# Attention with its split differences on VectorE, a shorter reciprocal square root and squares summed by ScalarE

## The chip, the cores and the metric

The kernel runs on one core of a Trainium2 chip. A core has a matrix engine (TensorE, PE in the profile; PEld is its weight load), three engines for arithmetic on whole tiles (VectorE or DVE, ScalarE or ACT, GpSimd or POOL) and a queue engine (SyncE, SP). Each works through its own instructions in order and waits on semaphores for the others. The metric is the device time of one execution in microseconds (us); lower is better.

## What is computed

Two layers over 512 tokens of width 1024, in fp32. Each layer is half a SwiGLU block, a mixer, and half a SwiGLU block, all behind RMS norms. The first mixer is a gated MLP. The second, which the change is about, is differential attention with 8 heads; every head has two queries and two keys of 64 and a value of 128:

```python
scores = jnp.einsum('bqhcd,bkhcd->bhcqk', qb, k).astype(jnp.float32) * scale   # scale = 64 ** -0.5
p = jax.nn.softmax(jnp.where(mask, scores, neg), axis=-1)
a = p[:, :, 0] - lam * p[:, :, 1]
o = jnp.einsum('bhqk,bkhe->bqhe', a, v)
...
o = rmsnorm(o, subln_g) * (1.0 - lambda_init)          # per head
return o.reshape(B, S, N_HEADS * V_DIM) @ w_o
```

with `rmsnorm(x, g) = x * rsqrt(mean(x*x) + 1e-6) * g`.

## The kernel before

Activations lie feature by token: 8 tiles `hT` of 128 features by 512 tokens. To keep fp32 accuracy at the speed of the fast matmul type, every operand is split: a rounded high part, copied by ScalarE (`split`, L166), and a low part, the operand minus its high part (L167). `mm3` (L171 to L173) then does three matmuls for a product: high by high, high by low, low by high. Weights come by DMA from the SP queue into `src` tiles and are split by `weights`, whose argument `engine` says who does the subtraction at L167: VectorE everywhere, except in attention, where three calls (the query weights `wq`, and both halves of the output weights `wo_b`) give it to GpSimd.

Stages run one after the other: a feed-forward block, the mixer, a feed-forward block, the projection of keys and values (`kv_proj`), a feed-forward block, attention, a last feed-forward block. At each border a `Norm` sums squares (GpSimd or VectorE, L217), `sums` brings them to 128 partitions with four small matmuls (`nps`, L222) and computes a reciprocal square root of 128 by 4 numbers with `rsqrt`, and `spread` broadcasts that with matmuls (`rps`, L234). `rsqrt` before: a shift (L179), a multiply-add (L182) and three Newton steps of three instructions (L187, L189, L193): eleven VectorE instructions. Apart from the border it is used once in the mixer, and once for each head in attention, in `subnorm`.

In `attention` the work is cut into 24 units: 8 heads by three groups of query blocks. The program is written as a loop over units with lags (`LAGS`), so that a unit's scores are issued while earlier units are transposed and multiplied by the values. Between them PE gets fill work: the query projections of the heads to come (`qps`, L171 to L173) and, late, the first half of the output projection (`dps`). For one head:

- `query`: VectorE scales the projection by the norm (L832) into one buffer `t1` (`r` in the rows; a ring of one place), ScalarE writes two high copies (L840, four casts of 64 by 512), GpSimd the low part `ql` (L841, two subtractions of 64 by 512).
- `scores`: matmuls into `sc` (L860, L865), a mask (L869), VectorE takes the row maxima (L877) and multiplies them by minus the scale (L879, `nm`), ScalarE takes the exponentials with their sums (L885), VectorE joins the two maps (L890, L892, L896, `pt`).
- `transposed` and `values`: PE transposes (`aps`, L907), ScalarE copies (L912), PE multiplies by the values into `ops` (L919).
- `subnorm`: ScalarE squares 128 by 512 (L930, `osq`), VectorE sums them (L932), divides twice by the softmax sum (L928, L935), scales (L938), does the eleven instructions of `rsqrt`, one product (L943, `rr`) and scales the output (L945, `on`).
- `headed`: PE transposes `on` (`otp`, L954), ScalarE and VectorE split the result (L956, L957).

A scheduler sets the order of the instructions on each engine from the order of the program and from durations of its own; a change of instructions can move others.

Of the kernel before, what the change touches and what calls it, by code (L numbers as in the profile page):

```python
# [9 lines left out]
F32 = mybir.dt.float32  # L10
# [7 lines left out]
P = 128  # L18
# [10 lines left out]
HD = 64  # L29
# [28 lines left out]
def trunk(ctx: ExitStack, tc: tile.TileContext, ins, out: bass.AP):  # L58
# [117 lines left out]
    def rsqrt(x, n, name, keep="ry"):  # L176
        y = sp.tile([P, n], F32, tag="ry", name=name, bufs=4)
        i = sp.tile([P, n], I32, tag="ri", name=name + "i")
        nc.vector.tensor_scalar(  # L179
            out=i, in0=x.bitcast(I32), scalar1=1, scalar2=None, op0=ALU.logical_shift_right  # L180
        )
        nc.vector.tensor_scalar(  # L182
            out=y.bitcast(I32), in0=i, scalar1=-1.0, scalar2=float(0x5F3759DF), op0=ALU.mult, op1=ALU.add
        )
        for step in range(3):
            a = sp.tile([P, n], F32, tag="ra", name=name + "a")
            nc.vector.tensor_tensor(out=a, in0=y, in1=y, op=ALU.mult)  # L187
            b = sp.tile([P, n], F32, tag="rb", name=name + "b")
            nc.vector.scalar_tensor_tensor(  # L189
                out=b, in0=a, scalar=-0.5, in1=x, op0=ALU.mult, op1=ALU.mult  # L190
            )
            z = sp.tile([P, n], F32, tag=keep if step == 2 else "ry", name=name + "z", bufs=4)
            nc.vector.scalar_tensor_tensor(  # L193
                out=z, in0=b, scalar=1.5, in1=y, op0=ALU.add, op1=ALU.mult
            )
            y = z
        return y
# [600 lines left out]
    def attention(nxt, kk, vv, rest, after):  # L798
        with phase("at", 2) as ap:
# [30 lines left out]
            def query(o):  # L830
                t1 = ring_1()
                nc.vector.tensor_tensor(out=t1, in0=o, in1=norm.rb, op=ALU.mult)  # L832
# [3 lines left out]
                for c in range(2):  # L836
# [4 lines left out]
                    nc.gpsimd.tensor_tensor(  # L841
# [5 lines left out]
            def scores(h, qis, l0):  # L847
# [24 lines left out]
                for slot, qi in enumerate(qis):  # L872
                    nk = (qi + 1) * P
                    ks = slice(slot * 256, slot * 256 + nk)
                    mx = sp.tile([P, 2], F32, tag="mx", name="mx")
                    for c, s in enumerate(sc):
                        nc.vector.tensor_reduce(out=mx[:, c : c + 1], in_=s[:, ks], axis=AX.X, op=ALU.max)  # L877
                    nm = sp.tile([P, 2], F32, tag="nm", name="nm")
                    nc.vector.tensor_scalar(  # L879
                        out=nm, in0=mx, scalar1=-(HD ** -0.5), scalar2=None, op0=ALU.mult  # L880
                    )
# [83 lines left out]
            def queries():  # L965

                for h in range(2, HEADS):
                    if h % 2 == 0:
                        pieces = weights(ins["wq"][h // 2], KD, engine=nc.gpsimd)
# [213 lines left out]
```

## Time and profile before

| | |
|---|---|
| median of 3 timed runs | 2111.07 us (2110.56 to 2114.93) |
| the profiled execution: time, span | 2116.63 us, 2114.5 us |
| PE busy, share of the span | 2049.0 us, 97% |
| VectorE busy | 1566.1 us, 74% |
| ScalarE busy | 917.4 us, 43% |
| GpSimd busy | 151.5 us, 7% |
| attention | from about 1575 us to 1735 us of the span |

[...]

### The profile page before, as it was taken

The numbers are of one execution on the slowest core, as the hardware profiler recorded it, in microseconds if no ns is written. First come the engines' busy times: TensorE is split into PE (matmuls) and PEld (weight loads), VectorE is DVE, ScalarE is ACT, GpSimd is POOL, SyncE is SP. The second block draws the span as 40 slices with busy tenths as digits, with TensorE's granted clock in tenths as the row PEclk, the third lists the DMA queues.
The fourth block names the chain that finished last, engine by engine and source line by source line (L and its number), as shares of the span: only waits on it lengthen the run. The fifth ranks groups of instructions, "written<-read, shape, count | busy, mean of one in ns | idle before, by whom it ended". The sixth has DMA issues, their size and how long they took to land.

```text
span 2114.5 us, 31293 instructions
## 1 busy us (share of the span) xinstructions
PE 2049.0 (97%) x12916; PEld 1839.1 (87%) x12916; DVE 1566.1 (74%) x2062; ACT 917.4 (43%) x1203; POOL 151.5 (7%) x131
## 2 busy tenths in 40 slices
PE   6999999999999999999998999999998999999997
PEld 6989898888888889899997899998976778989897
DVE  8868778447554688778688478696867978869687
ACT  6525345323232355335355245352546645525243
POOL 0000002004100000000002000000043320000000
PEclk9999999999999999999999999999998999999998
DMA  4422323332222232423223534242350021423231
GB/s 143 141 86 92 120 75 124 119 102 93 91 92 92 81 100 91 130 80 130 80 90 111 183 105 131 79 130 82 115 186 21 31 100 61 139 71 129 81 102 48
DMA packets 63439, 214.57 MB, mean 101 GB/s; under 512 B 7200, under 2 KB 9376, under 8 KB 63296
## 3 DMA queue, kind: packets, MB, share of 16 engines
q1 hardware_dynamic: 58752, 197.16, 28.5%
q0 software_dynamic: 4400, 15.34, 2.1%
q8 instruction: 101, 1.65, 0.3%
q14 instruction: 42, 0.34, 0.0%
q10 hardware_dynamic: 144, 0.07, 0.0%
HBM read 204.15 MB, written 8.39 MB: 101 GB/s over the span
## 4 chain that ended last, share of the span: by engine, by line
PE 69%; issue 18%; DVE 9%; ACT 2%; DMA 1%; POOL 0%; DVEq 0%; SPq 0%; POOLq 0%; ACTq 0%
PE ra L379 12%; PE rc L379 8%; PE dps L172 8%; PE dps L171 8%; PE dps L173 8%; PE rd L379 4%; PE rb L379 4%; PE ups L172 2%; PE ups L173 2%; PE vps L678 2%; PE ups L171 2%; PE vps L676 2%; PE vps L677 2%; DVE wlo L167 2%; PE sps L711 1%
## 5 line engine op out<-in xcount | busy, mean ns | idle before, releaser
L166 ACT CAST whi<-src 128x1024 fp32r<-128x1024 f32 (+2 forms) x500 | 513.3, 1034 | 870.2 <-PE dps L172 344.2
L167 DVE TENSOR_TENSOR wlo<-src,whi 128x1024 fp32r<-128x1024 f32 (+1 forms) x486 | 584.6, 1210 | 161.2 <-ACT whi L166 160.0
L379 PE MATMUL ra<-r,whi 128*128 128x256 f32 x2112 | 384.7, 282 | 14.8 <-ACT r L276 10.4
L172 PE MATMUL dps<-gl,whi 128*128 128x512 f32 x880 | 343.6, 391 | 2.9 <-DVE gl L167 2.9
L171 PE MATMUL dps<-gh,whi 128*128 128x512 f32 x880 | 344.4, 392 | 0.5 <-ACT r L912 0.4
L173 PE MATMUL dps<-gh,wlo 128*128 128x512 f32 x880 | 343.1, 390 | 0.0
L379 PEld LDWEIGHTS ra<-r,whi 128*128 128x128 f32 x2112 | 325.4, 189 | 19.1 <-ACT r L276 10.9
L379 PE MATMUL ra<-r,wlo 128*128 128x256 f32 x1056 | 296.9, 282 | 3.8 <-DVE wlo L167 3.7
L379 PE MATMUL rc<-r,whi 128*128 128x256 f32 x1408 | 255.1, 281 | 2.0 <-ACT whi L166 1.0
L370 DVE TENSOR_TENSOR src<-src 128x1024 f32<-128x1024 f32 x176 | 215.3, 1223 | 39.5 <-DMA src<-in_gu 36.1
L379 PEld LDWEIGHTS rc<-r,whi 128*128 128x128 f32 x1408 | 216.3, 189 | 4.5 <-DVE k L477 2.8
L379 PEld LDWEIGHTS ra<-r,wlo 128*128 128x128 f32 x1056 | 199.8, 189 | 5.7 <-DVE wlo L167 5.2
L172 PEld LDWEIGHTS dps<-gl,whi 128*128 128x128 f32 x880 | 166.0, 189 | 37.3 <-DVE gl L167 3.3
L379 PE MATMUL rc<-r,wlo 128*128 128x256 f32 x704 | 197.5, 280 | 0.9 <-DVE wlo L167 0.9
L171 PEld LDWEIGHTS dps<-gh,whi 128*128 128x128 f32 x880 | 165.6, 188 | 35.6 <-ACT gh L166 1.4
L173 PEld LDWEIGHTS dps<-gh,wlo 128*128 128x128 f32 x880 | 166.0, 189 | 34.5
L571 DVE TENSOR_TENSOR dps<-dps,rbh 128x512 f32<-128x512 f32 x88 | 61.3, 697 | 120.6 <-PE dps L173 120.5
L379 PEld LDWEIGHTS rc<-r,wlo 128*128 128x128 f32 x704 | 133.3, 189 | 1.1 <-DVE wlo L167 1.1
L379 PE MATMUL rd<-r,whi 128*128 128x256 f32 x704 | 129.4, 282 | 4.4 <-ACT r L276 2.1
L379 PE MATMUL rb<-r,whi 128*128 128x256 f32 x704 | 128.9, 282 | 0.4 <-ACT whi L166 0.4
L379 PEld LDWEIGHTS rd<-r,whi 128*128 128x128 f32 x704 | 108.9, 190 | 5.8 <-DVE r L277 2.5
L379 PEld LDWEIGHTS rb<-r,whi 128*128 128x128 f32 x704 | 109.3, 191 | 0.7 <-ACT whi L166 0.7
(239 smaller groups left out, 3159.6 us busy)
## 6 DMA issues: line engine op xcount, KB each, us to landing
src<-in_gu SPq DMA_DIRECT2D x176, 512.0 KB, 3.4
src<-in_dn SPq DMA_DIRECT2D x64, 512.0 KB, 4.6
src<-in_dn SPq DMA_DIRECT2D x32, 384.0 KB, 3.6
src<-in_wv SPq DMA_DIRECT2D x24, 512.0 KB, 3.5
src<-in_wu SPq DMA_DIRECT2D x24, 512.0 KB, 3.5
src<-in_wo_a SPq DMA_DIRECT2D x24, 512.0 KB, 3.5
src<-in_wk SPq DMA_DIRECT2D x8, 512.0 KB, 3.7
src<-in_wvv SPq DMA_DIRECT2D x8, 512.0 KB, 3.3
```

Of the source, the lines that this page charges most:

```text
L166: nc.scalar.copy(out=hi, in_=src)
L167: engine.tensor_tensor(out=lo, in0=src, in1=hi.bitcast(F32), op=ALU.subtract)
L171: nc.tensor.matmul(o, w[0], x[0], start=start, stop=False)
L172: nc.tensor.matmul(o, w[0], x[1], start=False, stop=False)
L173: nc.tensor.matmul(o, w[1], x[0], start=False, stop=stop)
L370: nc.vector.tensor_tensor(out=out, in0=a, in1=b, op=ALU.add)
L379: nc.tensor.matmul(o[:, a * H : (a + 1) * H], l[:, a, kp, :], r, start=first and kp == 0 and a == 0 and n == 0, stop=False, skip_group_che ...
L571: nc.vector.tensor_tensor(out=o, in0=o, in1=norm.rbh[:, tokens], op=ALU.mult)
L676: nc.tensor.matmul(acc[n], xh[:, ts], hi[:, kk, :], start=k == 0, stop=False)
L677: nc.tensor.matmul(acc[n], xh[:, ts], lo[:, kk, :], start=False, stop=False)
L678: nc.tensor.matmul(acc[n], xl[:, ts], hi[:, kk, :], start=False, stop=k == KD - 1)
L711: nc.tensor.matmul(sps[:, n * P : (n + 1) * P], v[ct // NCH * NCH + n][:, ct % NCH * P : (ct % NCH + 1) * P], wsT[:, gr, :], start=True, s ...
```

## The change

- The three weight loads of attention and the low part of the queries leave GpSimd for VectorE. GpSimd has no arithmetic left in attention.
- The scale of the scores moves from the maxima and the exponential into `query` (L832 becomes one instruction with two multiplications). The maxima are taken negated, straight into `nm`; the multiplication L879 falls away, 32 instructions.
- `rsqrt` takes eight instructions in place of eleven: a start by one multiply-add on the bits, one cubic step, one Newton step. This holds for every norm.
- `subnorm`: four squares of 128 by 128 with sums by ScalarE in place of one of 128 by 512 and a VectorE sum; the divisions by the softmax sum and the final product fall away, since the epsilon is multiplied by that sum squared instead (`el`, one instruction).

```diff
-    def rsqrt(x, n, name, keep="ry"):
-        y = sp.tile([P, n], F32, tag="ry", name=name, bufs=4)
-        i = sp.tile([P, n], I32, tag="ri", name=name + "i")
-        nc.vector.tensor_scalar(
-            out=i, in0=x.bitcast(I32), scalar1=1, scalar2=None, op0=ALU.logical_shift_right
+    C2, C1, C0 = 0.39755464, -1.29562372, 1.89804978
+
+    def rsqrt(x, n, name, keep="rr"):
...
+        y = step(
+            "ry",
+            lambda out: nc.vector.tensor_scalar(
+                out=out.bitcast(I32), in0=x.bitcast(I32), scalar1=-0.5, scalar2=float(0x5F350000),
+                op0=ALU.mult, op1=ALU.add,
+            ),
         )
-        nc.vector.tensor_scalar(
-            out=y.bitcast(I32), in0=i, scalar1=-1.0, scalar2=float(0x5F3759DF), op0=ALU.mult, op1=ALU.add
-        )
-        for step in range(3):
...
+        h = times(times(y, y, "ra"), x, "ra")
+        z = stt(stt(h, C1 / C2, h, ALU.add, "rb"), C0 / C2, y, ALU.add, "ry")
+        b = stt(times(z, z, "ra"), -0.5 * C2**3, x, ALU.mult, "rb")
+        return stt(b, 1.5 * C2, z, ALU.add, keep, bufs=4)
...
             def query(o):
                 t1 = ring_1()
-                nc.vector.tensor_tensor(out=t1, in0=o, in1=norm.rb, op=ALU.mult)
+
+                nc.vector.scalar_tensor_tensor(
+                    out=t1, in0=o, scalar=HD ** -0.5, in1=norm.rb, op0=ALU.mult, op1=ALU.mult
+                )
...
-                    nc.gpsimd.tensor_tensor(
+                    nc.vector.tensor_tensor(
                         out=ql[hs, :], in0=t1[hs, :], in1=qt[hs, :].bitcast(F32), op=ALU.subtract
                     )
...
-                    mx = sp.tile([P, 2], F32, tag="mx", name="mx")
+                    nm = sp.tile([P, 2], F32, tag="nm", name="nm")
                     for c, s in enumerate(sc):
-                        nc.vector.tensor_reduce(out=mx[:, c : c + 1], in_=s[:, ks], axis=AX.X, op=ALU.max)
-                    nm = sp.tile([P, 2], F32, tag="nm", name="nm")
-                    nc.vector.tensor_scalar(
-                        out=nm, in0=mx, scalar1=-(HD ** -0.5), scalar2=None, op0=ALU.mult
-                    )
+                        nc.vector.tensor_reduce(
+                            out=nm[:, c : c + 1], in_=s[:, ks], axis=AX.X, op=ALU.max, negate=True
+                        )
...
             def subnorm(o, l0):
 
-                rl = sp.tile([P, NCH], F32, tag="rl4", name="rl4")
-                nc.vector.reciprocal(out=rl, in_=l0)
+
                 sq = qp.tile([P, T], F32, tag="sq", name="osq").rearrange("p (n e) -> p n e", n=NCH)
-                nc.scalar.activation(out=sq.rearrange("p n e -> p (n e)"), in_=o, func=AF.Square)
                 ss = sp.tile([P, NCH], F32, tag="ss", name="ss")
-                nc.vector.tensor_reduce(out=ss, in_=sq, axis=AX.X, op=ALU.add)
-                for _ in range(2):
-                    st = sp.tile([P, NCH], F32, tag="ss", name="ss")
-                    nc.vector.tensor_tensor(out=st, in0=ss, in1=rl, op=ALU.mult)
-                    ss = st
+                for n in range(NCH):
+                    nc.scalar.activation(
+                        out=sq[:, n, :], in_=o[:, n * P : (n + 1) * P], func=AF.Square, accum_out=ss[:, n : n + 1]
+                    )
+                el = sp.tile([P, NCH], F32, tag="el", name="el")
+                nc.vector.scalar_tensor_tensor(
+                    out=el, in0=l0, scalar=RMS_EPS, in1=l0, op0=ALU.mult, op1=ALU.mult
+                )
...
-                r = rsqrt(ms, NCH, "or")
-                rr = sp.tile([P, NCH], F32, tag="rr", name="rr")
-                nc.vector.tensor_tensor(out=rr, in0=r, in1=rl, op=ALU.mult)
+                rr = rsqrt(ms, NCH, "or")
...
-                        pieces = weights(ins["wq"][h // 2], KD, engine=nc.gpsimd)
+                        pieces = weights(ins["wq"][h // 2], KD)
...
-                    for s, (hi, lo) in enumerate(weights(ins["wo_b"][0, dp], half, engine=nc.gpsimd)):
+                    for s, (hi, lo) in enumerate(weights(ins["wo_b"][0, dp], half)):
...
-                        ins["wo_b"][1, dp], half, engine=nc.gpsimd,
+                        ins["wo_b"][1, dp], half,
```

Where this moves instructions is shown at three places. The rows are an engine's instructions in order: line, operation, output and inputs, shape. Lines of the changed kernel are its own (after `rsqrt` they lie 8 to 11 higher).

The first place is VectorE at the end of the norm in the projection of keys and values. `nrz` and `nrrcol` are results of `rsqrt`; the last of them is what the matmuls `rps` on PE need. L267 to L277 and L275 to L285 prepare the next block. Before:

```order
L187 TENSOR_TENSOR nra<-nrz 128x4
L277 TENSOR_TENSOR r_10066<-spare,r_10066 128x768
L189 SCALAR_TENSOR_TENSOR nrb<-nra,ms 128x4
L277 TENSOR_TENSOR r_9978<-spare,r_9978 128x1024
L193 SCALAR_TENSOR_TENSOR nrz<-nrb,nrz 128x4
L167 TENSOR_TENSOR wlo<-src,whi 128x1024
L187 TENSOR_TENSOR nra<-nrz 128x4
L270 SCALAR_TENSOR_TENSOR spare<-spare 128x256
L189 SCALAR_TENSOR_TENSOR nrb<-nra,ms 128x4
L273 TENSOR_TENSOR spare<-spare 128x256
L193 SCALAR_TENSOR_TENSOR nrz<-nrb,nrz 128x4
```

The same place in the changed kernel:

```order
L185 TENSOR_TENSOR nrra<-nrry 128x4
L285 TENSOR_TENSOR r_10036<-spare,r_10036 128x768
L190 SCALAR_TENSOR_TENSOR nrrb<-nrra,ms 128x4
L285 TENSOR_TENSOR r_9948<-spare,r_9948 128x1024
L190 SCALAR_TENSOR_TENSOR nrrcol<-nrrb,nrry 128x4
L167 TENSOR_TENSOR wlo<-src,whi 128x1024
L278 SCALAR_TENSOR_TENSOR spare<-spare 128x256
L281 TENSOR_TENSOR spare<-spare 128x256
```

The result now stands where the second Newton step ended before; a weight subtraction and two steps of preparation come behind it.

The second place is VectorE in attention, where the first head's `on` is computed, for which PE's transposes `otp` wait. `or` to `orz` and `orry` to `orrr` are `rsqrt`, `mx` and `nm` the maxima, `pt` the joined maps. Before:

```order
L193 SCALAR_TENSOR_TENSOR orz<-orb,orz 128x4
L890 RECIPROCAL rl<-l_14183 128x1
L879 TENSOR_SCALAR nm<-mx 128x2
L187 TENSOR_TENSOR ora<-orz 128x4
L892 SCALAR_TENSOR_TENSOR r_14188<-l_14148,nl,rl 128x1
L189 SCALAR_TENSOR_TENSOR orb<-ora,oms 128x4
L832 TENSOR_TENSOR r_13642<-qps,rb 128x512
L193 SCALAR_TENSOR_TENSOR orz<-orb,orz 128x4
L896 SCALAR_TENSOR_TENSOR pt<-pt,r_14188 128x256
L943 TENSOR_TENSOR rr<-orz,rl_14104 128x4
L945 TENSOR_TENSOR on<-ops,rr 128x512
```

The same place in the changed kernel:

```order
L190 SCALAR_TENSOR_TENSOR orry<-orrb,orry 128x4
L898 RECIPROCAL rl<-l_14105 128x1
L888 TENSOR_REDUCE nm<-sc 128x1
L185 TENSOR_TENSOR orra<-orry 128x4
L900 SCALAR_TENSOR_TENSOR r_14110<-l_14086,nl,rl 128x1
L190 SCALAR_TENSOR_TENSOR orrb<-orra,oms 128x4
L904 SCALAR_TENSOR_TENSOR pt<-pt,r_14110 128x128
L190 SCALAR_TENSOR_TENSOR orrr<-orrb,orry 128x4
L898 RECIPROCAL rl<-l_14117 128x1
L952 TENSOR_TENSOR on<-ops,orrr 128x512
```

One Newton step, the product `rr` and the query's scaling are gone from in front of `on`, and `pt` of the second block now follows it.

The third place is VectorE late in attention, at the seventh head, where the split weights of the output projection (`wlo`, `k`) and the last query's low part (`ql`) now stand in its queue. Before:

```order
L879 TENSOR_SCALAR nm<-mx 128x2
L986 TENSOR_TENSOR h_76<-dps,h_76 128x512
L890 RECIPROCAL rl<-l_15033 128x1
L892 SCALAR_TENSOR_TENSOR r_15038<-l_14905,nl,rl 128x1
L928 RECIPROCAL rl_15289<-l_14905 128x4
L896 SCALAR_TENSOR_TENSOR pt<-pt,r_15038 128x512
L932 TENSOR_REDUCE ss<-osq 128x4
```

The same place in the changed kernel:

```order
L852 TENSOR_TENSOR ql<-r_13612,q_14871 64x512
L852 TENSOR_TENSOR ql<-r_13612,q_14875 64x512
L888 TENSOR_REDUCE nm<-sc 128x1
L993 TENSOR_TENSOR h_76<-dps,h_76 128x512
L167 TENSOR_TENSOR wlo<-src,whi 128x512
L898 RECIPROCAL rl<-l_14891 128x1
L167 TENSOR_TENSOR wlo<-src,whi 128x512
L900 SCALAR_TENSOR_TENSOR r_14896<-l_14771,nl,rl 128x1
L888 TENSOR_REDUCE nm<-sc 128x1
L904 SCALAR_TENSOR_TENSOR pt<-pt,r_14896 128x512
```

Two subtractions of 128 by 512 now stand in front of the head's `pt`, which PE transposes next.

## Rows read from the trace of the kernel before

**Rows 1.** Windows: us, busy us (instructions) per engine, PE clock, DMA share, GB/s.

```profile
1575.00:1735.00 160.00, 145.13 (x796) 113.42 (x796) 125.47 (x378) 91.70 (x225) 53.73 (x37) 0.94 0.16 53
1620.00:1700.00 80.00, 68.88 (x419) 53.01 (x418) 74.67 (x243) 52.55 (x140) 28.46 (x21) 0.98 0.11 38
1595.00:1610.00 15.00, 12.43 (x54) 8.94 (x53) 11.18 (x36) 10.41 (x32) 4.32 (x4) 0.66 0.06 19
1625.00:1635.00 10.00, 7.42 (x41) 5.46 (x42) 8.98 (x25) 6.04 (x14) 4.25 (x3) 0.83 0.08 28
1695.00:1710.00 15.00, 11.63 (x53) 8.76 (x52) 12.47 (x31) 8.32 (x21) 5.89 (x6) 0.77 0.42 137
1665.00:1670.00 5.00, 2.98 (x16) 2.01 (x15) 5.00 (x12) 3.86 (x9) 2.80 (x3) 1.00 0.16 54
1140.00:1155.00 15.00, 10.99 (x42) 8.89 (x41) 10.86 (x21) 7.09 (x10) 1.16 (x2) 0.77 0.38 130
```

**Rows 2.** Waits of PE, 1575 to 1735: us in total, times, longest.

```profile
PE otp L954 <- DVE rl L890: 5.5, 2, 3.5
PE otp L954 <- DVE on L945: 4.3, 2, 3.0
```

**Rows 3.** Timeline around one of these waits: start, us, instruction [idle before, releaser].

```profile
1624.21 2.48 POOL L167 TENSOR_TENSOR wlo<-src,whi 128x1024 fp32r<-128x1024 f32 x1 [8.18 <-PE ops L919]
1624.41 2.30 DVE L943 TENSOR_TENSOR rr<-orz,rl 128x4 f32<-128x4 f32 x1
...
1627.58 0.63 PE L954 MATMUL otp<-ident,on 128*128 128x128 f32 x4 [3.46 <-DVE rl L890]
```

**Rows 4.** L879: ns min/median/max; timeline, first and last held VectorE instruction.

```profile
L879 DVE TENSOR_SCALAR nm<-mx x32: 142/162/1643, 1593.8 to 1705.4; 128x2 f32<-128x2 f32 x32
...
1577.27 2.32 DVE L179 TENSOR_SCALAR nri<-ms 128x4 int32<-128x4 int32 x1
...
1712.63 1.21 DVE L189 SCALAR_TENSOR_TENSOR orb<-ora,oms 128x4 f32<-128x4 f32 x1
```

**Rows 5.** Groups of GpSimd, 1575 to 1735: busy us, mean ns | idle before.

```profile
L167 POOL TENSOR_TENSOR wlo<-src,whi 128x512 fp32r<-128x512 f32 (+1 forms) x13 | 22.6, 1741 | 56.3 <-ACT whi L166 32.4 <-PE otp L954 11.4 <-PE ops L919 8.2
L841 POOL TENSOR_TENSOR ql<-r,q 64x512 fp32r<-64x512 f32 x16 | 21.0, 1314 | 13.6 <-ACT q L840 9.9 <-PE sc L865 3.1
L167 POOL TENSOR_TENSOR k<-src,k 128x512 fp32r<-128x512 f32 x8 | 10.2, 1286 | 15.3 <-ACT k L166 15.2
```

**Rows 6.** VectorE: groups in attention and around it, and one row of the timeline.

```profile
1149.12 1.41 DVE L773 TENSOR_TENSOR kt<-t,kt 64x512 fp32r<-64x512 f32 x2
...
L167 DVE TENSOR_TENSOR wlo<-src,whi 128x1024 fp32r<-128x1024 f32 x3 | 3.7, 1224 | 0.2 <-ACT whi L166 0.2
...
L217 DVE TENSOR_TENSOR rb<-rb,sq 128x512 f32<-128x512 f32 x7 | 4.8, 685 | 0.0
...
L932 DVE TENSOR_REDUCE ss<-osq 128x4 f32<-128x512 f32 x8 | 5.4, 680 | 0.1
```

**Rows 7.** Groups of ScalarE by form, 1575 to 1735.

```profile
L885 ACT ACTIVATION_READ_ACCUMULATOR pt<-sc,nm 128x1 f32 x64 | 12.7, 198 | 0.0
...
L885 ACT ACTIVATE pt<-sc,nm 128x128 f32<-128x128 f32 x16 | 5.7, 363 | 7.9 <-PE sc L869 2.6 <-DVE r L892 1.8 <-DVE orz L193 1.2
...
L930 ACT ACTIVATE osq<-ops 128x512 f32<-128x512 f32 x8 | 4.9, 613 | 0.4 <-PE ops L919 0.4
```

**Rows 8.** Timeline of the norm in the projection of keys and values.

```profile
1142.68 0.15 DVE L193 SCALAR_TENSOR_TENSOR nrz<-nrb,nrz 128x4 f32<-128x4 f32 x1
...
1144.75 0.15 DVE L193 SCALAR_TENSOR_TENSOR nrz<-nrb,nrz 128x4 f32<-128x4 f32 x1
...
1144.96 2.08 PE L234 MATMUL rps<-ident,nrz 128*128 128x128 f32 x8 [4.00 <-DVE nrz L193]
```

**Rows 9.** Timeline of the last norm, at the end of the kernel.

```profile
2104.21 0.16 DVE L193 SCALAR_TENSOR_TENSOR nrz<-nrb,nrz 128x2 f32<-128x2 f32 x1
...
2104.79 0.16 DVE L193 SCALAR_TENSOR_TENSOR nrz<-nrb,nrz 128x2 f32<-128x2 f32 x1
```

More of the change, by code (lines that the diff above doesn't have):

```diff
@@ L173, in mm3, with step, times, stt @@
         nc.tensor.matmul(o, w[1], x[0], start=False, stop=stop)
-    def rsqrt(x, n, name, keep="ry"):
-        y = sp.tile([P, n], F32, tag="ry", name=name, bufs=4)
-        i = sp.tile([P, n], I32, tag="ri", name=name + "i")
-        nc.vector.tensor_scalar(
-            out=i, in0=x.bitcast(I32), scalar1=1, scalar2=None, op0=ALU.logical_shift_right
-        )
-        nc.vector.tensor_scalar(
-            out=y.bitcast(I32), in0=i, scalar1=-1.0, scalar2=float(0x5F3759DF), op0=ALU.mult, op1=ALU.add
-        )
-        for step in range(3):
[L186 to L190, printed above, removed]
-            )
[L192 to L197, printed above, removed]
+    C2, C1, C0 = 0.39755464, -1.29562372, 1.89804978
+    def rsqrt(x, n, name, keep="rr"):
+        def step(tag, f, **kw):
+            t = sp.tile([P, n], F32, tag=tag, name=name + tag, **kw)
+            f(out=t)
+            return t
+        def times(u, v, tag):
+            return step(tag, lambda out: nc.vector.tensor_tensor(out=out, in0=u, in1=v, op=ALU.mult))
+        def stt(u, c, v, op0, tag, **kw):
+            return step(
+                tag,
+                lambda out: nc.vector.scalar_tensor_tensor(out=out, in0=u, scalar=c, in1=v, op0=op0, op1=ALU.mult),
+                **kw,
+            )
[5 more added lines that the diff above has]
+            ),
+        )
+        h = times(times(y, y, "ra"), x, "ra")
+        z = stt(stt(h, C1 / C2, h, ALU.add, "rb"), C0 / C2, y, ALU.add, "ry")
+        b = stt(times(z, z, "ra"), -0.5 * C2**3, x, ALU.mult, "rb")
+        return stt(b, 1.5 * C2, z, ALU.add, keep, bufs=4)
     class Norm:
@@ L885, in scores @@
                         nc.scalar.activation(
-                            out=pt[:, c, :], in_=sc[c][:, ks], func=AF.Exp, bias=nm[:, c : c + 1],
-                            scale=HD ** -0.5, accum_out=ls,
+                            out=pt[:, c, :], in_=sc[c][:, ks], func=AF.Exp, bias=nm[:, c : c + 1], accum_out=ls
                         )
@@ L925, in subnorm @@
             def subnorm(o, l0):
[L927 to L928 removed]
                 sq = qp.tile([P, T], F32, tag="sq", name="osq").rearrange("p (n e) -> p n e", n=NCH)
[L930 removed]
                 ss = sp.tile([P, NCH], F32, tag="ss", name="ss")
[L932 to L936 removed]
+                for n in range(NCH):
[5 more added lines that the diff above has]
+                    out=el, in0=l0, scalar=RMS_EPS, in1=l0, op0=ALU.mult, op1=ALU.mult
+                )
                 ms = sp.tile([P, NCH], F32, tag="ms", name="oms")
[L938 to L943 removed]
+                nc.vector.scalar_tensor_tensor(
+                    out=ms, in0=ss, scalar=1.0 / P, in1=el, op0=ALU.mult, op1=ALU.add
+                )
+                rr = rsqrt(ms, NCH, "or")
                 on = qp.tile([P, T], F32, tag="sq", name="on").rearrange("p (n e) -> p n e", n=NCH)
```

3 lines of the change are left out of this document (removed).

## The prediction

> **What bounds the kernel now.** I read the busy time by stretch first, then PE's waits, then the rows around one wait. Over the span PE is busy 97% of the time, so only places where it stands still or runs at a lower clock are worth anything. Attention is the largest: of the 160 us from 1575 to 1735 PE is busy for 145.1, so it idles 14.9 us, and its mean clock is 0.94 [rows 1]. The loss to the clock sits in three stretches. In each I multiply PE's busy time by what the clock lacks: 12.43 x 0.34 = 4.2 us, 7.42 x 0.17 = 1.3 us and 11.63 x 0.23 = 2.7 us, together 8.2 us [rows 1]. In these three PE stands still for 2.6, 2.6 and 3.4 us; a stop of 2.02 us near 1667 was passed at full clock (1.00) [rows 1].
>
> What does PE wait for? 9.8 of the 14.9 us are waits of the transposes `otp` for VectorE, in four places [rows 2]. VectorE was busy 74.7 of the 80 us from 1620 to 1700, 93% [rows 1]; there it is the limit, though over the whole span it is busy only 74%. But part of that busy time is no work. At 1624.41 `rr`, a product of four numbers per partition, takes 2.30 us, and it ends when a GpSimd subtraction that began 0.2 us earlier ends (1624.21 + 2.48 = 1626.69); PE stops for 3.46 us [rows 3]. `nm` on two numbers takes 0.16 us in the median and up to 1.64 us [rows 4]. I went through VectorE's rows from 1575 to 1716 and took from each the shortest row of its line and shape: 26 of them are long, each beside a running GpSimd subtraction, with 26.2 us too much in all (the first and the last stand in [rows 4]; for the first, which has no equal in the stretch, I took 0.16). So **GpSimd's arithmetic holds VectorE**, which costs about as much as if VectorE had done the work.
>
> **The change part by part.** First VectorE's account in attention, against its 125.5 us [rows 1].
>
> Away: the 26.2 us held. The 32 `nm` at 0.16 us, 5.1 us [rows 4]. The eight sums of squares, 5.4 us [rows 6]. For each head seven small instructions go (one reciprocal, two divisions, three of `rsqrt`, the product `rr`) and one comes (`el`): 48 in all, and three more in the norm at the border, at 0.16 us as in [rows 9]: 8.2 us.
>
> New: 16 subtractions of 64 by 512 for `ql`. The same operation and shape on VectorE took 1.41 us for two in the key projection [rows 6], so 11.3 us against 21.0 us on GpSimd [rows 5]. Of the 13 `wlo` in the stretch five are 128 by 1024, at 1.22 us, and eight are 128 by 512, as are the eight `k`, at 0.685 us [rows 5, 6]: 6.1 + 11.0 us. Together 28.4 us.
>
> The balance is 125.5 - 26.2 - 5.1 - 5.4 - 8.2 + 28.4 = 109.0 us. VectorE gets lighter by 16 us though it takes over all of GpSimd's work. The multiplication by the scale in `query` rides on an instruction that is there already, and the negation on the maximum; no row shows either form. I take nothing; if the second pass of the scale cost as much as one small instruction, 0.16 us, eight would be 1.3 us, hidden beside PE's fill work.
>
> ScalarE: one square of 0.613 us per head becomes four of 128 by 128. The nearest rows are the exponentials of that shape, 0.363 us, and the reading of their sums, 0.198 us [rows 7]. These overlap, so four cost between 4 x 0.363 = 1.45 and 4 x 0.561 = 2.24 us, 6.7 to 13.0 us more for eight heads. ScalarE then has 98 to 105 of 160 us: no bound. On the way to `on` the longer squares (0.8 to 1.6 us) stand against the dropped sum (0.68 us [rows 6]) and six small instructions (1.0 us), so the way gets no longer. [...]
>
> PE's waits: with 109 us of work in front of PE's 145, VectorE no longer sets the pace, but it still works in order, so some waits stay. In the wait of 3.46 us the hold was 2.30 - 0.16 = 2.14 us, 62% [rows 3]. At that share 9.2 of the 14.9 us go with the holds alone; all 14.9 is the other end. New in front of PE are the weight subtractions, thickest at the sixth and seventh head, where two stand ahead of `pt` (1.4 us) in place of a held row or two (1.1 us each). I take **10.9 us**, and leave 4.0 us of waits, because the tail of `rsqrt` is also shorter.
>
> Clock: with stops below 2 us the drops should not come, as near 1667 [rows 1]. Of 8.2 us I take **6 us**, as if one of the two smaller drops stayed in part; the ends are 0 and 8.2.
>
> Projection of keys and values: PE stops 4.00 us for the last step of `rsqrt`, which starts at 1144.75; in the changed order the result stands in the place that started at 1142.68 [rows 8]. So **2.07 us** go and a stop of 1.93 us is left. Behind the stop the clock cost 10.99 x 0.23 = 2.5 us [rows 1]; 1.93 is below the 2.02 that was passed at full clock, so I take the **2.5 us** too (bounds 0 and 2.5).
>
> End of the kernel: nothing runs beside the last norm, and three of its steps 0.19 us apart (2104.21 to 2104.79) go [rows 9]: **0.6 us**. The other norms are covered by matmuls, but for half a microsecond at two borders, which I leave as reserve. The SP queue's order does not change; the weights' buffers come free earlier with VectorE at 0.685 in place of 1.29 us, which no one waits for.
>
> Sum: 10.9 + 6 + 2.07 + 2.5 + 0.6 = 22 us, against the profiled execution's 2116.63 us. That execution is 5.6 us above the median. Stops that fall differently against the clock are the only part of it that I can see vary, so I assume that the median pays less of the clock's 8.5 us, and count 18 us there: **2093 us**.
>
> **The rivals.** *VectorE becomes the bound, slower.* If VectorE's held time was time in which it would have waited anyway, taking the hold away gives nothing, and its queue in attention grows by 28.4 - 5.1 - 5.4 - 8.2 = 9.7 us. It decides from the point where less than 9.7 of the 26.2 us held come back as time. For it: the late heads, where the `wlo` and `k` now stand in front of `pt`. Against it: VectorE was 93% busy around the holds, and in [rows 3] the held instruction itself was what PE waited for. If all of it lands on the path: 2111 + 10 = 2121 us. [...]
>
> *The waits only change their name, no difference.* PE's order in attention is fixed, and `otp` may wait for squares or casts instead of VectorE. ScalarE gets up to 13 us more. Then the 14.9 us and the clock's loss stay, and only 2.07 + 0.6 us come: 2108 us.
>
> *Half of it.* The waits shrink to about half, but each is still long enough for the clock to fall: 5.5 of the 14.9 us, and 2.07 + 0.6, about 8 us: 2103 us.
>
> *Everything goes.* 14.9 + 8.2 + 2.07 + 2.5 + 0.6 = 28 us: 2083 us. This is the lower end of the forecast, no case of its own.
>
> **How the numbers follow.** Forecast (9 to 28 us gained) 0.70; half of it (4.2 to 9) 0.12; no difference 0.11; slower 0.07. A measurement of this kernel can tell about 0.2% from no change, 4.2 us. Faster by more than that: 0.70 + 0.12 = 0.82. The range takes the forecast and the half, 2083 to 2107 us.
>
> **What would show it.** Right: from 1575 to 1735 no small VectorE instruction above 0.3 us; VectorE busy at about 109 us in that stage; GpSimd idle there; PE's `otp` waits below 2 us each and its clock at 1.00 through attention; the `rps` wait in the key projection at about 1.9 us with the clock at 1.00 behind it; three steps fewer at the end. Wrong: VectorE at 95% in the late heads with `aps` or `otp` waiting for `pt` or `on` behind `wlo`; `osq` as the releaser of `on`; maxima that cost more negated than plain; or the same waits without any hold, which would say that latency and not VectorE's load set them.

## The result, and the profile after

| | before | changed |
|---|---|---|
| median of 4 runs, us | 2113.0 (2110.56 to 2115.86) | 2083.1 (2082.27 to 2086.65) |
| profiled execution: time, span, us | 2116.63, 2114.5 | 2086.65, 2084.9 |
| ratio of the times (95% interval) | | 0.9861 (0.9842 to 0.9881) |

The changed kernel is faster by 29.9 us. The direction and the places were right and the range held the time, but only by 0.1 us at its lower end: 2093 was 10 us too high, and that the range held is luck in part. These are the span and the busy times of the changed kernel's page:

```profile
span 2084.9 us, 31172 instructions
...
PE 2039.0 (98%) x12916; PEld 1835.3 (88%) x12916; DVE 1547.1 (74%) x1985; ACT 922.0 (44%) x1259; POOL 95.1 (5%) x93
```

Attention is where most of it came from. The busy time by stretch, in the order of [rows 1], for the changed kernel: first the whole stage with its borders, then from the first matmul into `sc` to the last `otp`.

```profile
1570.00:1705.00 135.00, 134.26 (x792) 107.08 (x791) 108.42 (x322) 96.17 (x281) 0.00 (x0) 1.00 0.19 63
1584.00:1704.00 120.00, 119.26 (x716) 94.62 (x717) 101.29 (x304) 89.53 (x273) 0.00 (x0) 1.00 0.18 60
```

The second of these stretches in the kernel before:

```profile
1589.00:1732.00 143.00, 128.60 (x715) 99.46 (x714) 117.80 (x360) 84.92 (x216) 46.39 (x33) 0.93 0.15 51
```

PE's idle time fell from 143.00 - 128.60 = 14.4 us to 0.7 us, and for the same matmuls its busy time fell by 128.60 - 119.26 = 9.3 us, because the clock is now 1.00 throughout, where it was 0.93 on average. That is 23 us in one stage. PE's waits there (us in total, times, longest), where [rows 2] had two of 5.5 and 4.3 us:

```profile
PE ops L927 <- ACT r L920: 0.7, 1, 0.7
```

Three groups of VectorE and two of ScalarE in the changed kernel, 1570 to 1705 (busy us, mean ns | idle before):

```profile
L888 DVE TENSOR_REDUCE nm<-sc 128x1 f32<-128x128 f32 (+3 forms) x64 | 30.6, 482 | 1.1 <-PE sc L880 0.7 <-ACT pt L894 0.2
...
L852 DVE TENSOR_TENSOR ql<-r,q 64x512 fp32r<-64x512 f32 x16 | 11.0, 685 | 3.3 <-ACT q L851 2.2 <-PE sc L876 0.6
...
L167 DVE TENSOR_TENSOR k<-src,k 128x512 fp32r<-128x512 f32 x8 | 5.4, 686 | 0.0
```

```profile
L939 ACT ACTIVATE osq<-ops 128x128 f32<-128x128 f32 x32 | 8.6, 289 | 0.9 <-PE ops L927 0.8
...
L939 ACT ACTIVATION_READ_ACCUMULATOR osq<-ops 128x1 f32 x32 | 7.0, 219 | 0.0
```

The second place is the norm in the projection of keys and values. In the changed kernel:

```profile
1131.84 1.05 PE L230 MATMUL nps<-ones,rb 128*128 128x1 f32 x8 [0.40 <-POOL rb L225]
...
1140.40 1.81 PE L242 MATMUL rps<-ident,nrrcol 128*128 128x128 f32 x8 [1.94 <-DVE nrrcol L190]
```

The first of these rows in the kernel before; the second stands in [rows 8]:

```profile
1134.33 1.05 PE L222 MATMUL nps<-ones,rb 128*128 128x1 f32 x8 [0.42 <-POOL rb L217]
```

From `nps` to `rps` it took 1144.96 - 1134.33 = 10.63 us and now takes 1140.40 - 1131.84 = 8.56 us.

Summed over the span (29.6 us), cut at the first matmuls of the stages: attention 23.3 us (143.5 to 120.2), the projection of keys and values 3.0 us (98.4 to 95.4), the feed-forward block ahead of it 4.7 us (344.1 to 339.4). The first block got longer by 2.6 us (356.0 to 358.6). It scatters: over all kernels it takes 356.0 to 357.5 us with the old `rsqrt` and 356.8 to 358.8 us with the new one, so the new one may cost about 1 us there; the ranges overlap. All else together is 1.2 us.

### The profile page after: what moved, and what is told of

It reads as the page before. It is cut to its first block, busy times and chain, and to the rows that moved or that the text cites. A ratio compares the mean times of both kernels' runs of the same rounds, so it can differ in the third digit from the quotient of the medians.

```text
span 2084.9 us, 31172 instructions
## 1 busy us (share of the span) xinstructions
PE 2039.0 (98%) x12916; PEld 1835.3 (88%) x12916; DVE 1547.1 (74%) x1985; ACT 922.0 (44%) x1259; POOL 95.1 (5%) x93
## 4 chain that ended last, share of the span: by engine, by line
PE 74%; issue 18%; DVE 6%; ACT 1%; DMA 1%; POOL 0%; DVEq 0%; POOLq 0%; ACTq 0%
PE ra L387 13%; PE rc L387 8%; PE dps L172 8%; PE dps L171 8%; PE dps L173 8%; PE rd L387 4%; PE rb L387 4%; PE ups L172 2%; PE vps L686 2%; PE ups L171 2%; PE ups L173 2%; PE vps L684 2%; PE vps L685 2%; DVE wlo L167 1%; PE sps L719 1%
## 5 line engine op out<-in xcount | busy, mean ns | idle before, releaser
L167 DVE TENSOR_TENSOR wlo<-src,whi 128x1024 fp32r<-128x1024 f32 (+2 forms) x500 | 597.9, 1203 | 164.7 <-ACT whi L166 159.7
```

Source lines behind the costliest of these rows:

```text
L167: engine.tensor_tensor(out=lo, in0=src, in1=hi.bitcast(F32), op=ALU.subtract)
```

## Experiments: the move and the arithmetic apart

The length of attention below goes from the start of the first matmul into `sc` to the end of the last `otp`, as both stand in the timeline: before 143.5 us, changed 120.2 us. It is that of one execution of each kernel. "Held" rows are counted as in the prediction: VectorE rows more than 0.2 us above the shortest of their line and shape; this count covers a slightly other stretch than the prediction's and gives 25 rows and 24.0 us for the kernel before. The ratios are to the kernel before on the same chip, whose median was 2111.25 to 2112.37 us beside the experiments.

One thing has to be kept in mind in all of them. The prediction says that "PE's order in attention is fixed"; it is not. The scheduler places the fill work and the transposes anew when VectorE's instructions change. Of the 717 matmuls of this stretch, 128 places hold another product (by output and shape) in the changed kernel than before, 235 in the move alone, 86 in the arithmetic alone. Only the kernel with extra work on GpSimd has the order of the changed kernel in every place. In the others, a part of a difference can come from the order; no run holds the order fixed there.

**Only the move**: the kernel before, with its four kinds of GpSimd subtractions on VectorE.

```diff
-                    nc.gpsimd.tensor_tensor(
+                    nc.vector.tensor_tensor(
                         out=ql[hs, :], in0=t1[hs, :], in1=qt[hs, :].bitcast(F32), op=ALU.subtract
...
-                        pieces = weights(ins["wq"][h // 2], KD, engine=nc.gpsimd)
+                        pieces = weights(ins["wq"][h // 2], KD)
...
-                    for s, (hi, lo) in enumerate(weights(ins["wo_b"][0, dp], half, engine=nc.gpsimd)):
+                    for s, (hi, lo) in enumerate(weights(ins["wo_b"][0, dp], half)):
...
-                        ins["wo_b"][1, dp], half, engine=nc.gpsimd,
+                        ins["wo_b"][1, dp], half,
```

> The kernel before with its GpSimd subtractions in attention moved to VectorE and nothing else. VectorE in attention: 125.5 - 26.2 held + 28.4 new = 127.7 us, about what it was. Theory H: no instruction of a few numbers takes over 0.3 us any more, but VectorE is as full as before, so PE's waits fall only in part: 2098 to 2110 us. Rival L: more instructions on a full engine, 2113 to 2123 us.

**Only the arithmetic**: the changed kernel with the same subtractions back on GpSimd, the diff above the other way round.

> The changed kernel with the three weight subtractions and the queries' low parts back on GpSimd: the rewritten arithmetic alone. Theory H (GpSimd's arithmetic holds VectorE, and the holds set PE's waits): the 37 GpSimd subtractions still hold VectorE, some 20 us in attention, so PE's waits there stay at 5 us or more and one or two drops of the clock stay: 2095 to 2107 us. Rival L (VectorE simply had too many instructions; 18.7 us fewer are what helps): 2083 to 2090 us.

Measured: the move alone 2105.56 us (0.997, 0.9959 to 0.998), the arithmetic alone 2088.42 us (0.9892, 0.9877 to 0.9907). Attention, the move alone, then the arithmetic alone:

```profile
1587.00:1722.00 135.00, 126.20 (x718) 98.42 (x717) 112.72 (x392) 84.99 (x217) 0.00 (x0) 0.96 0.16 54
```

```profile
1579.00:1708.00 129.00, 123.01 (x719) 96.92 (x718) 96.40 (x272) 89.55 (x272) 46.75 (x33) 0.97 0.17 56
```

Two small groups in the move alone (ns min/median/max), which [rows 3, 4] showed held for up to 2.30 us:

```profile
L943 DVE TENSOR_TENSOR rr<-orz,rl x8: 148/158/164, 1617.1 to 1712.6; 128x4 f32<-128x4 f32 x8
...
L879 DVE TENSOR_SCALAR nm<-mx x32: 139/159/168, 1590.5 to 1690.9; 128x2 f32<-128x2 f32 x32
```

With no held row left, the move alone still leaves PE idle for 8.8 us, at a clock of 0.96, and attention takes 135.1 us: 8.4 us gained. Its time lies in theory H's range. With 15 rows held for 13.6 us, the arithmetic alone leaves 6.0 us idle, and attention takes 128.8 us: 14.7 us gained. Its time lies in the range of rival L, not in that of theory H; the holds, the idle time and a drop of the clock are there as theory H said, but they cost less. The two gains add up to 23.1 of the 23.3 us, so the rewritten arithmetic brought more of attention's gain than the move. It does not follow that holds mattered little: with fewer small rows to hold, the arithmetic alone also cut the held time by 24.0 - 13.6 = 10.4 us, about half of the 117.80 - 96.40 = 21.4 us that it took off VectorE. The two kernels separate the halves of the edit, not held time from work.

**Half of the move**: the changed kernel with only `ql`, then with only the weights back on GpSimd, each by its lines of the diff above.

> The changed kernel with the queries' low parts alone (16 subtractions of 64 by 512, 1.31 us each) on GpSimd. Theory H: about half of the holds come back, 8 to 12 us on VectorE, and go against 11.3 us of work that leaves it: VectorE keeps its total, but waits come back at the places held: 2084 to 2092 us. Rival L: VectorE has 11 us less, 2080 to 2083 us.

> The changed kernel with the split of the weights in attention alone on GpSimd (21 subtractions, 33 us there). Theory H: holds of 10 to 15 us come back, up to 2.3 us at a time, against 17 us of work that leaves VectorE: 2085 to 2094 us, with PE waiting for a held row. Rival L: 2080 to 2083 us.

Measured: `ql` on GpSimd 2084.65 us (0.9874, 0.986 to 0.9889), attention 122.3 us; the weights on GpSimd 2090.63 us (0.9898, 0.9881 to 0.9914), attention 126.4 us. Both times lie in theory H's ranges. The intervals of `ql` and of the changed kernel overlap, so the moved `ql` is worth little by itself; the weights are worth about 6 us of attention. That stage with the weights on GpSimd:

```profile
1585.00:1711.00 126.00, 119.21 (x716) 94.08 (x715) 105.21 (x285) 88.95 (x272) 28.45 (x19) 1.00 0.18 57
```

Here 14 rows are held for 14.7 us, and all that is lost is PE's idle time of 6.8 us; the clock stays at 1.00.

## Experiments: what a hold costs, and how much room VectorE has

**Extra work on GpSimd**: the changed kernel with 32 subtractions of 128 by 512 on GpSimd that no one reads. The order of the instructions of all other engines is that of the changed kernel.

```diff
+            scr = ap.tile([P, T], F32, tag="scr", name="scr", bufs=1)
+            nc.vector.memset(scr, 1.0)
...
-                    rl = sp.tile([P, 1], F32, tag="rl", name="rl")
+                    rl = sp.tile([P, 1], F32, tag="rl", name="rl", bufs=8)
                     nc.vector.reciprocal(out=rl, in_=l2)
+                    nc.gpsimd.tensor_tensor(
+                        out=scr, in0=scr, in1=rl.broadcast_to([P, T]), op=ALU.subtract
+                    )
```

> The changed kernel with 32 extra GpSimd subtractions of 128 by 512, one behind each reciprocal of the joined maps, into a scratch tile that nothing reads. The order of every other engine is that of the changed kernel. About 32 x 1.29 = 41 us of GpSimd. Theory H (a running GpSimd subtraction holds VectorE): 15 to 25 us of holds on VectorE's instructions of a few numbers, and attention 4 to 15 us longer: 2087 to 2098 us. Rival (GpSimd runs beside VectorE at no cost): 2083 us, no VectorE instruction of a few numbers above 0.3 us.

**The same work on VectorE**, 32 subtractions, and then 16 of them (behind every second `rl`).

```diff
-                    nc.gpsimd.tensor_tensor(
+                    nc.vector.tensor_tensor(
                         out=scr, in0=scr, in1=rl.broadcast_to([P, T]), op=ALU.subtract
```

> The same 32 subtractions on VectorE instead, 32 x 0.685 = 22 us more there. If VectorE has room left beside PE in the changed kernel, 2083 to 2088 us. If its load sets the pace from there on, the 22 us bring it above PE's time in attention: 2095 to 2110 us. Against the kernel with the same subtractions on GpSimd this tells which of the two costs more, work on VectorE or a hold by GpSimd.

> The changed kernel with 16 extra subtractions of 128 by 512 on VectorE in attention, 11 us, in place of 32 (which made attention 15.6 us longer for 22 us of work). If VectorE has room for some of it beside PE: attention 0 to 4 us longer, 2083 to 2088 us. If the cost is proportional from the first microsecond on: 7 to 8 us longer, 2090 to 2092 us.

| | time, us | ratio (95%) | attention, us |
|---|---|---|---|
| changed kernel | 2083.1 | 0.9861 (0.9842 to 0.9881) | 120.2 |
| 32 more on GpSimd | 2094.17 | 0.9911 (0.9896 to 0.9926) | 133.6 |
| 32 more on VectorE | 2096.62 | 0.9924 (0.991 to 0.9939) | 135.9 |
| 16 more on VectorE | 2084.11 | 0.9867 (0.985 to 0.9884) | 122.6 |

The hold itself, with extra work on GpSimd, in the timeline (start, us, instruction):

```profile
1621.18 1.04 POOL L901 TENSOR_TENSOR scr<-scr,rl 128x512 f32<-128x512 f32 x1 [0.84 <-DVE rl L900]
1621.28 0.96 DVE L197 TENSOR_SCALAR orry<-oms 128x4 int32<-128x4 int32 x1
```

The VectorE row on four numbers ends where the GpSimd row ends (1622.24 and 1622.22), as in [rows 3]. Two lines of the same kernel (ns min/median/max, first and last start):

```profile
L901 POOL TENSOR_TENSOR scr<-scr,rl x32: 1038/1040/1519, 1584.9 to 1690.6; 128x512 f32<-128x512 f32 x32
...
L905 DVE SCALAR_TENSOR_TENSOR r<-l,nl,rl x32: 205/426/1083, 1585.0 to 1691.0; 128x1 f32<-128x1 f32 x32
```

The line of `r` in the changed kernel, and the extra rows on VectorE in the kernel with all 32 there:

```profile
L900 DVE SCALAR_TENSOR_TENSOR r<-l,nl,rl x32: 206/214/227, 1589.1 to 1680.3; 128x1 f32<-128x1 f32 x32
```

```profile
L901 DVE TENSOR_TENSOR scr<-scr,rl x32: 675/683/689, 1588.4 to 1695.4; 128x512 f32<-128x512 f32 x32
```

25 of the 30 held rows end 0.01 to 0.02 us from the end of a GpSimd row. 32 x 1.04 = 33.3 us of GpSimd hold the 30 rows for 20.2 us and cost 13.3 us of attention, with the order of all other engines unchanged. Five of the held rows are large ones, `pt` of up to 128 by 512. Done by VectorE, the same work takes 32 x 0.683 = 21.9 us and costs 15.6 us. So the mechanism that the prediction read from [rows 3] stands, and its price too: here holds cost VectorE 20.2 us, about what the work itself would have cost it. One hold may have gone the other way as well: one GpSimd row took 1.519 us, 0.48 us more than the median; it began 0.07 us behind a VectorE subtraction of 0.69 us. The row `on`, which reads a matmul's result, took 0.673 to 0.692 us in all eight cases, as without the extra work (0.672 to 0.692); four of the eight ran beside a GpSimd row. Why these were not held, while L197 on four numbers took 0.96 us, no run here shows.

How much room VectorE has, the last two kernels show. Attention with 16 more, then with 32 more:

```profile
1582.00:1705.00 123.00, 121.23 (x720) 95.24 (x719) 108.38 (x321) 90.09 (x272) 0.00 (x0) 1.00 0.17 59
```

```profile
1583.00:1719.00 136.00, 127.39 (x719) 98.07 (x718) 117.77 (x336) 90.38 (x273) 0.00 (x0) 0.97 0.16 53
```

The first 11 us of extra work cost 2.3 us, the next 11 cost 13.3 us. A price in proportion to the load falls; it looks like an edge. Up to it PE's fill work covers VectorE, and PE stands still for 123.00 - 121.23 = 1.8 us at a clock of 1.00; beyond it PE stands still for 8.6 us, and the clock falls too, to 0.97. PE is also busy 127.39 - 119.26 = 8.1 us longer; by the prediction's measure, busy time times what the clock lacks, the clock accounts for 127.39 x 0.03 = 3.8 us of it, and what the rest is no run separates.

That VectorE's load alone makes the edge is not shown. PE's order differs from the changed kernel's in 133 places with 16 more and in 297 with 32 more, and VectorE is busy 88% of the stage with 16 more (108.38 of 123.00 us) and 87% with 32 more (117.77 of 136.00 us). The other 16 also stand behind other blocks. So the order, or the place of the extra work, remains a rival.

## Experiments: the parts of the arithmetic

**One part alone, on the kernel before**: the negated maxima with the scale in `query`; the eight-operation `rsqrt`; the squares summed by ScalarE with `el` in place of the divisions (and the old `rsqrt`). Each takes its piece of the diff of the change and nothing else.

> The kernel before with the negated maxima and the scale in the query, nothing else: 32 instructions of 0.16 us fewer, 5.1 us, and with them the 6.5 us for which GpSimd held them (11.6 us for 32 against 0.16 each). All the arithmetic together took 29 us off VectorE in attention and 14.7 us off its length, about half a microsecond for each. Theory N (a microsecond off VectorE is worth that, whatever it is): 8 to 12 us off VectorE, attention 4 to 6 us shorter: 2105 to 2109 us. Rival (the maxima count more, as the exponentials wait for them): 2098 to 2105 us.

> The kernel before with the eight-instruction reciprocal square root and nothing else. Outside attention as in the changed kernel: 3 to 5 us in the projection of keys and values, 2 to 4 us in the block before it, half a microsecond at the end. In attention 24 instructions of 0.16 us fewer and the holds on them: theory N gives 2 to 4 us there: 2101 to 2107 us. Rival (only the norms at the borders count): 2105 to 2109 us.

> The kernel before with the new squares and the epsilon times the sum squared, with the eleven-instruction reciprocal square root: 8 sums of 0.68 us and 32 - 8 small instructions fewer on VectorE, 9 us, and 5 to 6 us of holds (rr and the two divisions): theory N gives 5 to 8 us in attention: 2104 to 2108 us. Rival (ScalarE's longer squares eat it): 2110 to 2113 us.

**One part undone, in the changed kernel**: the old eleven-operation `rsqrt`; one square of 128 by 512 and a sum by VectorE.

```diff
-                for n in range(NCH):
-                    nc.scalar.activation(
-                        out=sq[:, n, :], in_=o[:, n * P : (n + 1) * P], func=AF.Square, accum_out=ss[:, n : n + 1]
-                    )
+                nc.scalar.activation(out=sq.rearrange("p n e -> p (n e)"), in_=o, func=AF.Square)
+                nc.vector.tensor_reduce(out=ss, in_=sq, axis=AX.X, op=ALU.add)
```

> The changed kernel with the eleven-instruction reciprocal square root in every norm. From the trace: the projection of keys and values 2 to 3 us longer, the feed-forward block in front of it 2 to 5 us longer, 0.6 us at the end, and in attention 24 instructions of 0.16 us on VectorE with the tail of each head's norm longer, 0 to 5 us: 2088 to 2096 us. If VectorE has room in attention and only its load counts, nothing there: 2086 to 2089 us.

> The changed kernel with one square of 128 by 512 on ScalarE and the sum of squares on VectorE again, 5.4 us more on VectorE and 7 to 13 us less on ScalarE. If VectorE's load sets what is left: 2084 to 2088 us. If ScalarE's four squares cost their place in its queue: 2080 to 2083 us.

| | time, us | ratio (95%) | attention, us |
|---|---|---|---|
| maxima alone | 2105.68 | 0.9969 (0.9956 to 0.9982) | 137.1 |
| `rsqrt` alone | 2102.31 | 0.9954 (0.9939 to 0.9969) | 137.0 |
| squares and `el` alone | 2105.54 | 0.997 (0.9957 to 0.9982) | 137.2 |
| changed, old `rsqrt` | 2090.29 | 0.9892 (0.9878 to 0.9907) | 120.6 |
| changed, one square | 2086.66 | 0.9878 (0.9861 to 0.9894) | 121.4 |

Each part alone takes 6.3 to 6.5 us off attention, 19.2 us in all, where the three together took 14.7 us. Undone in the changed kernel, the `rsqrt` costs attention 0.4 us and the square 1.1 us. That fits an edge: a kernel short of it hardly notices some more work. In attention, neither of these two was needed for itself; the maxima were not undone alone. That the three overlap is not explained by an edge: 143.5 - 19.2 = 124.3 us would still lie above the changed kernel's 120.2. The square's time lies in the range for VectorE's load, but its four runs, 2082.41 to 2087.32 us, reach into both ranges.

The new `rsqrt` has worth outside attention. With the old one in the changed kernel the projection of keys and values takes 98.3 us again (95.4), the block ahead of it 341.1 us (339.4), and `nps` to `rps` 10.63 us (8.56).

That all three come to nearly the same gain I cannot explain. Their times lie in theory N's ranges, but theory N falls. From 117.80 us before, VectorE's busy time in the stage goes down by 8.5 us with the maxima, 6.4 with the `rsqrt` and 14.1 with the squares, so a microsecond is not always worth the same. The 29 us from which theory N was drawn compared stretches of 160 and 129 us; over the same stage it is the 21.4 us given above. The mix differs too: maxima alone, `rsqrt` alone, then squares and `el` alone:

```profile
1585.00:1722.00 137.00, 124.91 (x717) 98.00 (x717) 109.31 (x328) 85.82 (x217) 47.26 (x33) 0.96 0.16 53
```

```profile
1583.00:1720.00 137.00, 125.47 (x717) 97.87 (x717) 111.38 (x336) 84.92 (x216) 45.83 (x34) 0.96 0.16 53
```

```profile
1584.00:1721.00 137.00, 128.56 (x717) 100.69 (x716) 103.71 (x328) 88.56 (x272) 46.39 (x33) 0.93 0.16 53
```

In the first PE idles 12.1 us and is busy 5.7 us longer than the changed kernel's 119.26, in the last it idles 8.4 us and is busy 9.3 us longer, at a clock of 0.93.

## Why the prediction was right, and where it was off

**Holds and VectorE's account: right.** The forecast was 109.0 us for the stage, the trace has 108.4. Of the unknown forms the negated maxima cost 482 ns on average, the plain ones of before 480; `query` with two multiplications takes 686 ns, as with one. `ql` at 0.685 us and `k` at 0.686 us are as priced from [rows 5, 6]. In attention GpSimd is idle, and no row is held. ScalarE has 96.2 us over this stretch, just under the forecast's 98 to 105, because the squares were priced too high. A square took 0.289 us and the reading of its sum 0.219 us, but they overlap. The busy time of all these rows over the stage:

```profile
1570.00:1705.00 135.00, 9.69 (x64) 1.00 0.19 63
```

That is 1.21 us for the four squares of a head, below the bounds of 1.45 to 2.24 us from [rows 7], and for eight heads 9.69 - 4.9 = 4.8 us more than before, not 6.7 to 13.0.

**PE's waits in attention: the size was off.** The step that failed is "leave 4.0 us of waits": 0.7 us were left, so that 14.4 - 0.7 = 13.7 us came and not 10.9. The share of 62% from one wait was too simple as well: it gave 9.2 us for the holds alone, and the move alone took only 14.4 - 8.8 = 5.6 us off PE's idle time. The rest came with the arithmetic, which the prediction counted in VectorE's balance and then gave little of the waits.

**Clock in attention: the size was off.** 6 of 8.2 us were taken; 9.3 us came. The step that failed is the product of PE's busy time and the mean clock of a stretch. The three stretches of [rows 1] hold all of the loss, and between them the clock is 1.00. But each of them mixes time at 1.00, where most of PE's idle time lies, with time at 0.50, where PE was busy for 88 to 100% of it. Cut at the level of the clock, the kernel before shows:

```profile
1597.50:1607.70 10.20, 9.44 (x32) 6.75 (x32) 7.77 (x26) 7.51 (x23) 2.61 (x2) 0.50 0.01 2
1607.70:1628.20 20.50, 17.04 (x113) 13.59 (x112) 16.64 (x53) 13.66 (x36) 7.42 (x4) 1.00 0.06 20
1628.20:1631.60 3.40, 3.40 (x13) 2.16 (x12) 3.25 (x7) 3.28 (x6) 1.73 (x2) 0.51 0.10 38
1631.60:1699.90 68.30, 60.75 (x375) 46.79 (x373) 63.54 (x210) 44.80 (x122) 24.19 (x19) 1.00 0.12 40
1699.90:1706.70 6.80, 5.98 (x18) 4.25 (x19) 5.79 (x12) 3.35 (x9) 2.57 (x3) 0.50 0.31 86
```

Matmuls of `qps`, 128 by 512, start 0.42 us apart from 1630.84 to 1631.68, at the end of the stretch at 0.51, and 0.23 to 0.24 us apart right behind it, at 1.00. With half of the busy time counted as lost at 0.50, the loss is an estimated (9.44 + 3.40 + 5.98) / 2 = 9.4 us. The reason given, that shorter stops would no longer pull the clock down, agrees with the changed kernel, whose longest stop there is 0.7 us; the last section has kernels in which it fails.

**Projection of keys and values: the stop exact, the clock behind it wrong.** 2.07 us were forecast and 10.63 - 8.56 = 2.07 us came; a stop of 1.93 us was forecast and 1.94 us is there. But the 2.5 us of the clock behind it came only in part: the stage gained 3.0 us, 0.9 us beyond the stop. The step that failed is "1.93 is below the 2.02 that was passed at full clock". The changed kernel by 2 us, before, in and behind its stop:

```profile
1132.00:1134.00 2.00, 2.00 (x14) 1.78 (x15) 2.00 (x7) 0.98 (x2) 0.00 (x0) 1.00 0.37 129
...
1138.00:1140.00 2.00, 0.46 (x3) 0.04 (x1) 2.00 (x5) 1.47 (x2) 0.00 (x0) 1.00 0.31 123
...
1142.00:1144.00 2.00, 2.00 (x6) 1.61 (x6) 1.36 (x3) 1.71 (x3) 0.00 (x0) 0.50 0.71 213
```

Behind the stop the clock is at 0.50. The kernel with 32 more subtractions on GpSimd, whose program is the same here, 1.45 us earlier in its span:

```profile
1132.00:1134.00 2.00, 2.00 (x6) 1.57 (x5) 2.00 (x5) 2.00 (x3) 0.00 (x0) 0.50 0.00 0
...
1138.00:1140.00 2.00, 1.69 (x12) 1.24 (x11) 1.36 (x3) 1.04 (x1) 0.00 (x0) 1.00 0.00 0
```

The matmuls `nps` and `rps` of the same kernel:

```profile
1130.39 1.05 PE L230 MATMUL nps<-ones,rb 128*128 128x1 f32 x8 [0.40 <-POOL rb L225]
...
1138.95 1.16 PE L242 MATMUL rps<-ident,nrrcol 128*128 128x128 f32 x8 [0.31 <-DVE nrrcol L190]
```

Here the clock fell ahead, beside the fill work, to 0.50. PE then needed longer for it, arrived later and waited 0.31 us. From `nps` to `rps` it is again 8.56 us, so in this kernel VectorE's chain of small instructions sets that length, and the clock ahead of it costs nothing; with the full clock behind, the stage takes 93.8 us and not 95.4. The arithmetic alone shows the same 8.56 us and 93.8 us.

It is not always so. With 32 more subtractions on VectorE the clock is at 0.50 ahead of `rps` for longer; the way takes 9.46 us, `rps` does not wait for VectorE, and the stage takes 94.6 us:

```profile
1133.00:1139.00 6.00, 5.89 (x18) 5.02 (x19) 5.53 (x13) 3.67 (x5) 0.06 (x1) 0.50 0.19 61
```

With the old `rsqrt`, in the move, the maxima and the squares alone, the way takes 11.4 us and not 10.63. In the move alone the clock was lower ahead: the matmuls of the fill work, 128 by 512, started 0.43 us apart from 1133.70 to 1136.26 and 0.23 us apart behind that. In that kernel VectorE also waits inside the chain, for the high part of a weight:

```profile
1141.02 1.23 DVE L167 TENSOR_TENSOR wlo<-src,whi 128x1024 fp32r<-128x1024 f32 x1 [0.64 <-ACT whi L166]
```

In the new order this subtraction stands behind the last instruction of the chain.

**End of the kernel: right for the wait, lost in the scatter of one pair.** The last `rps` waits 1.82 us; before it waited 2.42:

```profile
2075.43 1.23 PE L242 MATMUL rps<-ident,nrrcol 128*128 128x128 f32 x4 [1.82 <-DVE nrrcol L190]
```

```profile
2105.01 1.22 PE L234 MATMUL rps<-ident,nrz 128*128 128x128 f32 x4 [2.42 <-DVE nrz L193]
```

The way from the last `fps` to the end of these matmuls shrank only from 7.04 to 6.96 us in this pair. Over all kernels it is 7.0 to 7.4 us in the five with the old `rsqrt` and 6.4 to 7.0 us in the nine with the new one, on average 7.22 and 6.67 us, which is close to the forecast 0.6 us.

**Left out.** The block ahead of the projection of keys and values takes 340.98 to 341.22 us in every later kernel with the old `rsqrt` and 339.18 to 339.50 us in every one with the new: 1.7 us, which the prediction left "as reserve" at two borders. The other 3 us of that block's 4.7 lie in the profile of before alone, whose block was longer than in any later kernel with the same code there.

**From the profiled execution to the median.** The step that failed is the discount, "count 18 us there". It took 4 of the 5.6 us by which the profiled execution lay above the median for a loss to the clock that only this execution had. But the changed kernel's profiled execution lies 3.6 us above its median too, and that of before 3.6 us above its median of four. The difference of the profiled executions, 30.0 us, and of the medians, 29.9 us, agree. Without the discount the same sum would have said 2089 us.

**The rivals.** VectorE as the bound, slower: it falls, but VectorE is not far from it. If load makes the edge, it lies between 11 and 22 us of work more than the changed kernel has; the 28.4 us that moved onto VectorE came with 26.2 us of holds and 18.7 us of work taken off it. No difference: it falls, as the only wait left for ScalarE is 0.7 us, and PE's order, from which it argued, was not fixed. Half of it: it falls; the move alone, another kernel, comes near its 2103 us with 2105.56. "Everything goes" at 2083 us came true, in part for other reasons: more clock in attention, less behind the projection's norm, and a border that was not counted.

What stays open: why the parts alone gain nearly the same; how much of attention's gain comes from PE's new order; and where exactly the edge lies and whether load alone makes it, as each attention length is that of one execution. None of these kernels beats the changed one: `ql` on GpSimd, 16 more subtractions and one square have medians 1.0 to 3.6 us above it, with overlapping intervals.

## What to carry to other kernels

Where small VectorE rows end together with a GpSimd row, count the held time as VectorE's own work: handing arithmetic to GpSimd relieved little or nothing here (32 more subtractions cost attention 13.3 us on GpSimd and 15.6 us on VectorE; the weights on GpSimd made it 6.2 us longer). Ask how far the loaded engine is from the point at which its partner begins to wait: here each of three parts gained over 6 us in attention while PE waited much, and two of them undone cost 0.4 and 1.1 us where it waited 0.7 us. At a border that waits for a chain of small dependent instructions, take the length of the chain as the term, not the stop, since the stop changes with the clock of the work beside it (of 8.56 us, the stop was 1.94 us with that work at 1.00 and 0.31 us with part of it at 0.50); and look for what stands inside the chain and waits for others. Before a load is called the cause, compare the order of the engine that waits: here only one experiment left it as it was.

## What the runs showed of the hardware that was not expected

Here the length of one stop did not tell whether the clock fell. A stop of 1.94 us was followed by 0.50, one of 2.02 us was passed at 1.00 [rows 1]; with the weights on GpSimd PE idled 6.8 us in attention, at most 2.0 us at a time, at 1.00 throughout, while 8.8 us idle in the move alone, at most 1.8 us at a time, went with 0.96. And one and the same piece of program, around the norm of the keys and values, ran ahead of its stop at 1.00 in one kernel and at 0.50 in another, after the same `nps` with the same 0.40 us of waiting.
